# Hybrid decoder block: x2's place as weight buffer twice, the last pair's down in five parts, final_g by DMA, first gate behind two gather groups

## The chip, the cores and the metric

One core of a Trainium2 chip runs the whole program. The metric is the device time of one execution in microseconds; several executions are timed and their median counts. A profile is one execution of its own, with a span (first to last instruction) a little shorter than its device time.

## The reference

One decoder layer on 512 tokens of width 2048, in float32: an attention block (sliding-window heads and forgetting-attention heads) and then a mixture of experts. What matters here is the second half:

```
h2 = rmsnorm(x1, g_moe) * (1 + scale) + shift
group  = top-1 of 4 groups;  expert = top-2 of the 8 experts of that group     # per token
y_e    = (silu(h2 @ w_gate[e]) * (h2 @ w_up[e])) @ w_down[e]                   # 32 experts, 2048 -> 512 -> 2048
x2     = x1 + gate_moe * sum over the token's two experts of weight * y_e
out    = rmsnorm(x2, final_g)
```

The weights of all 32 experts are read once, 12.6 MB for an expert, 403 MB in all.

## The kernel before

The attention block and the router come first. Then 32 experts run in 16 pairs (class `Pair`): the two experts of a pair have up to 64 token slots each and lie side by side in TensorE's columns. Two pairs make a duo (class `Duo`), 8 duos in all. `run_duos` writes the order out by hand, and each engine works in the order of the program.

For a duo the tokens are gathered by matmuls with one-hot matrices (`gather`, tile `xe`), in eight groups of 256 columns of the width. Each group needs its 256 columns of the normed tokens split into a high and a low part first (`split_x`; ScalarE makes the high part, VectorE the low one). The four blocks of a split wait in the list `cuts`, and `step()` runs one of them behind every quarter of a half gate_up; `gather(h)` runs what is left of group h, and at its end asks for the split of a later group. The first duo has three places for splits, so group h + 3 is asked for at the end of gather h.

`gate_up(cc)` multiplies a quarter cc of the width with gate (`pg`, L1345) and up (`pu`), eight matmul pairs each; quarter cc needs groups 2cc and 2cc + 1. In the first duo the order is: gathers 0, 1, 2; gate 0, gather 3, up 0, gather 4; gate 1, gather 5, up 1, gather 6; gate 2, gather 7, up 2; gate 3, up 3. Then `act` and `hid_T` make the hidden rows, `down_rows` (L1367) multiplies them with the down weights, and the sums go back to their tokens by matmuls with the one-hot matrices (`scatter4`, L1389), which VectorE adds into x2 (L1392). The scatters of a pair run between the gate_ups of the next.

Weights come as tiles of [128, 4, 512] float32, 1024 KB: 16 for gate and up and 8 for down in a pair, numbered n = 0 to 383 in the order of their loads. `wload` issues them on SP's queue, a pair ahead of its use, and a load waits until the last reader of its buffer is done. `ring_tile` gives the buffers: two pools of four (`mo`, `rp_`) in turn. Tiles 8 to 11 (quarter 2 of the first pair) take the place of x2, which is not written before the second pair. So tiles 12 to 15 wait for quarter 0, 16 to 19 for quarter 1, 20 to 23 for quarter 3 and so on. All loads are in one queue, in order.

The last pair differs. Its down weights come by column blocks (`down_src`, pieces of 2 KB), the last block in halves. `down` (L1404) multiplies a part of columns (512, 512, 512, 256, 256) with them, VectorE scales it by `gm` (L1409), ScalarE copies the high part (L1414), VectorE makes the remainder (L1415), and four scatters (`scatter`, L1427) for the four token blocks wait in the list `late`; behind each k of the next part `step()` runs one. VectorE adds into x2 (L1429) and ScalarE sums the squares (`last_norm`, L1593). When the last square is in, the root is taken and x2 is scaled with it and with final_g (`fg`, L1604) and stored (L1605). `fg` needs the 2048 values on all 128 partitions: they are loaded as 16 rows of 128 (`fgs`, on ScalarE's queue, at the start of the experts) and spread by 32 matmuls with 16 rows (`fgp`, L1587) and four copies, behind quarter 1 of the last pair.

Of the kernel before, what the change touches and what calls it, by code (L numbers as in the profile page):

```python
# [8 lines left out]
F32 = mybir.dt.float32  # L9
# [8 lines left out]
D = 2048  # L18
TB = 4
# [34 lines left out]
def kernel(  # L54
# [1140 lines left out]
    early = rp_.tile([128, TB, D], F32, tag="x2", name="early")  # L1195
# [81 lines left out]
    def ring_tile():  # L1277

        n = nld[0]
        nld[0] += 1  # L1280
        if 8 <= n < 12:
            return early[:, n - 8, :].rearrange("p (k f) -> p k f", k=4)
        k = n if n < 8 else n - 4
        return (mo, rp_)[k // 4 % 2].tile([128, 4, 512], F32, tag="w", name=f"w{n}", bufs=4)
# [19 lines left out]
    class Pair:  # L1304
# [78 lines left out]
        def scatter4(self, dc, tbs=range(TB)):  # L1383

            sl = slice(dc * 512, (dc + 1) * 512)
            os_ = [ps.tile([128, 512], F32, tag="y", name=f"o_{self.n}_{dc}_{tb}", bufs=4) for tb in tbs]
            for o, tb in zip(os_, tbs):
                for i, v in enumerate(YP[dc % 2]):
                    PE.matmul(o, self.ohT[:, tb, :], v, start=i == 0, stop=i == 1)  # L1389
            for o, tb in zip(os_, tbs):  # L1390
                x2 = total()[:, tb, sl]
                V.scalar_tensor_tensor(x2, o, self.w_col(tb), x2 if self.n else x1[dc][:, tb, :], op0=OP.mult,  # L1392
                                       op1=OP.add)
            if dc < 2 and tbs[-1] == TB - 1:
                self.prepare(dc + 2)

        def down(self, c0, c1):

            dc, sl, w = c0 // 512, slice(c0 % 512, c0 % 512 + c1 - c0), c1 - c0
            name = f"{self.n}_{c0}"  # L1400
            y = ps.tile([128, 512], F32, tag="y", name=f"y_{name}", bufs=4)[:, :w]
            for k in range(4):
# [3 lines left out]
                if 512 <= c0 < 1536:  # L1406
                    step()
            yt = YT[dc % 2][:, sl]
            V.tensor_mul(yt, y, gm[:, c0:c1])  # L1409
            if c1 == D:  # L1410
                parts = (yt,)
            else:
                hi, lo = (t[:, CHUNKS.index((c0, c1)) % 2, :w] for t in XP)
                S.activation(hi, yt, AF.Copy)  # L1414
                V.tensor_sub(lo, yt, hi.bitcast(F32))  # L1415
                parts = (hi, lo)
            if c0 == 1536:
                for _ in range(TB):
                    step()
            late.extend(lambda tb=tb: self.scatter(c0, c1, tb, parts) for tb in range(TB))  # L1420

        def scatter(self, c0, c1, tb, parts):
            o = ps.tile([128, 512], F32, tag="g" if tb % 2 else "y", name=f"o_{self.n}_{c0}_{tb}",
                        bufs=2 if tb % 2 else 4)[:, :c1 - c0]
            oh = self.ohT[:, tb, :]
            for i, v in enumerate(parts):
                PE.matmul(o, oh if len(parts) > 1 else oh.bitcast(F32), v, start=i == 0, stop=i == len(parts) - 1)  # L1427
            x2 = total()[:, tb, c0:c1]
            V.scalar_tensor_tensor(x2, o, self.w_col(tb), x2, op0=OP.mult, op1=OP.add)  # L1429
            self.done((c0, c1), tb)  # L1430
# [63 lines left out]
    def total():  # L1494

        if not x2s:
            x2s.append(rp_.tile([128, TB, D], F32, tag="x2", name="x2"))
        return x2s[0]
# [3 lines left out]
    late, cuts = [], []  # L1502
# [5 lines left out]
    def step():  # L1508

        if late:  # L1510
            late.pop(0)()
        if cuts:
            cut()

    def run_duos(duos, done=None, after=None):
# [3 lines left out]
        for n, (duo, q) in enumerate(order):  # L1519
# [6 lines left out]
            p.done = done if final else None  # L1526
            nxt = duos[duos.index(duo) + 1] if q and not final else None
            if own:
                for h in range(3):
                    duo.gather(h)  # L1530
# [3 lines left out]
            for cc in range(4):  # L1534
                if own:
                    p.gate_up(cc, lambda: duo.gather(2 * cc + 3) if cc < 3 else None)
                    if cc < 2:
                        duo.gather(2 * cc + 4)
# [13 lines left out]
                if cc == 1 and p.done:  # L1552
                    done(None)
# [7 lines left out]
            if p.done:  # L1561
                for cols in CHUNKS:
                    p.down(*cols)
                while late:
                    step()
                return
# [9 lines left out]
    fgs = sm([16, 128], "fgs")  # L1576
    S.dma_start(fgs, final_g.rearrange("(r f) -> r f", r=16))
# [4 lines left out]
    def last_norm(cols, tb=0):  # L1582
        if cols is None:
            for r in range(4):
                t = ps.tile([128, 512], F32, tag="g", name=f"fgp_{r}", bufs=2)
                for k in range(4):
                    PE.matmul(t[:, k * 128:(k + 1) * 128], ident[0:16, 4 * r + k:4 * r + k + 1].to_broadcast([16, 128]),  # L1587
                              fgs, start=True, stop=True)
                S.activation(fg[:, r * 512:(r + 1) * 512], t, AF.Copy)
# [3 lines left out]
        S.activation(HID[:, :c1 - c0], total()[:, tb, c0:c1], AF.Square, accum_out=sf5[:, tb, i:i + 1])  # L1593
# [5 lines left out]
        for tb in range(TB):  # L1599
            y = ring_tile()  # L1600
            for h in range(2):
                sl = slice(h * 1024, (h + 1) * 1024)
                yv = flat(y)[:, sl]
                V.scalar_tensor_tensor(yv, total()[:, tb, sl], rf[:, tb:tb + 1], fg[:, sl], op0=OP.mult, op1=OP.mult)  # L1604
# [114 lines left out]
```

## Time and profile before

| | us |
|---|---|
| three runs | 1917.44, 1919.84, 1924.72 (median 1919.84) |
| profiled execution, device time | 1920.35 |
| its span | 1918.7 |
| TensorE busy in the span | 1811.1 (94%) |
| weight loads of TensorE | 1136.6 (59%) |
| VectorE, ScalarE, GpSimd | 1064.2, 773.5, 342.1 |
| moved by DMA | 572.79 MB |

The mean granted clock of TensorE is 0.981 of full speed. Busy shares are means over stages with different limits; the stages must be read one by one. In the views below, PE is TensorE's matmuls, PEld its weight loads, DVE VectorE, ACT ScalarE, SPq the queue on which SP issues DMAs. L1345 is line 1345 of the kernel. A matmul in the timeline has a start and a modelled end; the spacing of the starts tells more than the durations.

### The profile page before, as it was taken

To read this page: it belongs to the slowest core of one execution; us is meant where nothing else is said; L and a number is where in the kernel's file an instruction comes from. 1 tells how busy PE (TensorE), PEld (TensorE's weight loads), DVE (VectorE), ACT (ScalarE), POOL (GpSimd) and SP (SyncE) were. 2 spreads that over 40 slices of the span, in tenths; PEclk is the share of its full clock that TensorE was granted. 3 is DMA by queue.
4 is the path that set the end of the run, shared out by engine and by line. 5 is a ranking of instruction groups with operands and counts; after the bars stand their busy time and mean duration, and the time that the engine had idled before them with its cause. 6 is when DMAs were issued, how large, how long until landed. Compare 5 with 4: busy or idle time off the path is not lost.

```text
span 1918.7 us, 26373 instructions
## 1 busy us (share of the span) xinstructions
PE 1811.1 (94%) x9801; PEld 1136.6 (59%) x9801; DVE 1064.2 (55%) x1904; ACT 773.5 (40%) x1523; POOL 342.1 (18%) x281
## 2 busy tenths in 40 slices
PE   4998999999999999997999999999999999999994
PEld 2667888787787777776544454444544445444442
DVE  5774666566666545756445455554545545455425
ACT  4445655565555533345423233232332323323113
POOL 2440343443344321454000000000000000000000
PEclk9999999999999899999999999999999999999998
DMA  9993555565566432668699999999999999999993
GB/s 329 325 291 80 162 175 156 163 201 163 170 179 190 120 133 77 216 219 322 234 397 419 421 419 421 420 418 420 418 421 421 417 420 417 421 420 413 421 393 119
DMA packets 208680, 572.79 MB, mean 299 GB/s; under 512 B 22624, under 2 KB 110744, under 8 KB 159904
## 3 DMA queue, kind: packets, MB, share of 16 engines
q1 hardware_dynamic: 207600, 570.95, 79.2%
q8 instruction: 79, 1.29, 0.3%
q14 instruction: 57, 0.47, 0.1%
q10 hardware_dynamic: 944, 0.08, 0.0%
HBM read 566.78 MB, written 4.19 MB: 298 GB/s over the span
## 4 chain that ended last, share of the span: by engine, by line
PE 68%; DMA 7%; ACT 7%; DVE 6%; issue 3%; POOL 1%; SPq 0%; DVEq 0%; ACTq 0%; POOLq 0%
PE pu L1345 11%; PE pg L1345 10%; PE y L1367 9%; PE xe L1479 7%; PE o L1389 5%; DMA w<-in_w_up_dram 5%; PE qp L213 3%; PE qp L215 2%; PE qp L214 2%; DMA raw<-in_w_ada_dram 2%; PE ob L824 1%; PE tb L812 1%; PE vb L214 1%; PE vb L215 1%; PE vb L213 1%
## 5 line engine op out<-in xcount | busy, mean ns | idle before, releaser
L1345 PE MATMUL pu<-w,cw 128*64 128x512 f32 x1008 | 235.9, 593 | 5.9 <-DMA w<-in_w_up_dram 5.9
L1345 PE MATMUL pg<-w,cw 128*64 128x512 f32 x1008 | 235.1, 604 | 0.0
L1488 ACT ACTIVATE cw<-xe,shM,scM 128x128 f32<-128x128 f32 x128 | 58.5, 457 | 427.5 <-PE xe L1479 396.5
L1367 PE MATMUL y<-w,more_f 128*64 128x512 f32 x960 | 217.4, 599 | 4.5 <-ACT xp_whi L1460 2.4
L1486 DVE TENSOR_SCALAR cw<-xe,scM,shM 128x128 f32<-128x128 f32 x128 | 52.5, 410 | 296.9 <-ACT cw L1488 296.9
L623 POOL TENSOR_TENSOR gb<-gb,raw 128x512 f32<-128x512 f32 x112 | 159.6, 1425 | 275.6 <-ACT raw L622 207.2
L1392 DVE SCALAR_TENSOR_TENSOR x<-o,wpair,x 128x512 f32<-128x512 f32 x240 | 163.2, 742 | 26.6 <-PE o L1389 26.6
L1345 PEld LDWEIGHTS pu<-w,cw 128*64 128x64 f32 x1008 | 75.8, 137 | 151.9 <-issue 137.6
L1460 ACT ACTIVATE xp_whi<-x,rs 128x256 fp32r<-128x256 f32 x236 | 162.4, 761 | 1.1 <-DVE rs L133 1.1
L1367 PEld LDWEIGHTS y<-w,more_f 128*64 128x64 f32 x960 | 74.4, 137 | 135.0 <-issue 106.6
L175 DVE TENSOR_TENSOR wlo_s<-raw,whi_s 128x512 fp32r<-128x512 f32 x96 | 89.9, 937 | 109.6 <-ACT whi_s L174 109.5
L1345 PEld LDWEIGHTS pg<-w,cw 128*64 128x64 f32 x1008 | 71.8, 138 | 130.8 <-issue 128.2
L1466 DVE SCALAR_TENSOR_TENSOR xp_wlo<-x,rs,xp_whi 128x256 fp32r<-128x256 f32 x232 | 144.9, 684 | 2.2 <-ACT xp_whi L1460 2.2
L1479 PE MATMUL xe<-cr,xp_whi 128*128 128x256 f32 x472 | 119.8, 294 | 2.4 <-DVE cr L1449 2.4
L620 DVE SCALAR_TENSOR_TENSOR ga<-raw,csil,ga 128x512 f32<-128x512 f32 x112 | 107.9, 963 | 23.1 <-DMA raw<-in_w_ada_dram 22.7
L1479 PEld LDWEIGHTS xe<-cr,xp_whi 128*128 128x128 f32 x472 | 89.8, 190 | 49.5 <-issue 45.4
L1479 PE MATMUL xe<-cr,xp_wlo 128*128 128x256 f32 x472 | 113.7, 281 | 0.3
L213 PE MATMUL qp<-hT_hi,whi_s 128*128 128x512 f32 x256 | 107.3, 419 | 0.0
L215 PE MATMUL qp<-hT_hi,wlo_s 128*128 128x512 f32 x256 | 100.8, 394 | 0.0
L214 PE MATMUL qp<-hT_lo,whi_s 128*128 128x512 f32 x256 | 100.8, 394 | 0.0
L622 ACT ACTIVATE raw<-raw,csil 128x512 f32<-128x512 f32 x112 | 79.7, 714 | 32.1 <-DMA raw<-in_w_ada_dram 23.5
L1479 PEld LDWEIGHTS xe<-cr,xp_wlo 128*128 128x128 f32 x472 | 90.0, 191 | 0.7 <-DVE xp_wlo L1466 0.7
(451 smaller groups left out, 3512.2 us busy)
## 6 DMA issues: line engine op xcount, KB each, us to landing
w<-in_w_gate_dram SPq DMA_DIRECT2D x126, 1024.0 KB, 4.9
w<-in_w_up_dram SPq DMA_DIRECT2D x126, 1024.0 KB, 13.5
w<-in_w_down_dram SPq DMA_DIRECT2D x126, 1024.0 KB, 12.3
raw<-in_w_ada_dram SPq DMA_DIRECT2D x128, 512.0 KB, 4.4
raws<-in_w_ada_dram SPq DMA_DIRECT2D x64, 512.0 KB, 7.0
raw<-in_w_in_dram SPq DMA_DIRECT2D x160, 128.0 KB, 3.0
raw<-in_w_out_dram SPq DMA_DIRECT2D x32, 512.0 KB, 3.8
raw<-in_w_in_dram SPq DMA_DIRECT2D x48, 256.0 KB, 3.4
```

Source lines behind the costliest of these rows:

```text
L213: PE.matmul(o, lhi, rhi, start=first, stop=False, **kw)
L214: PE.matmul(o, lhi, rlo, start=False, stop=False, **kw)
L215: PE.matmul(o, llo, rhi, start=False, stop=last, **kw)
L620: V.scalar_tensor_tensor(a, ts[n][:, j, :], s, a, op0=OP.mult, op1=OP.add)
L623: G.tensor_add(a, a, ts[n][:, j, :])
L1345: PE.matmul(o[64 * e:64 * e + 64, :], self.xe(cc)[:, j, 64 * e:64 * e + 64], w[cc, e][:, j, :], start=cc == 0 and j == 0, stop=cc == 3 and ...
L1367: PE.matmul(ys[dc][64 * e:64 * e + 64, :], HT[:, k, 64 * e:64 * e + 64], self.wd[k, e][:, dc, :], start=k == 0, stop=k == 3)
L1389: PE.matmul(o, self.ohT[:, tb, :], v, start=i == 0, stop=i == 1)
L1392: V.scalar_tensor_tensor(x2, o, self.w_col(tb), x2 if self.n else x1[dc][:, tb, :], op0=OP.mult, op1=OP.add)
L1460: S.activation(hi[tb], xv, AF.Identity, scale=s)
L1466: V.scalar_tensor_tensor(lo[tb], xv, s, hi[tb].bitcast(F32), op0=OP.mult, op1=OP.subtract)
L1479: PE.matmul(t[:, j, :], v[tb][:, j, :], OHS[:, tb].rearrange("p q s -> p (q s)"), start=tb + i == 0, stop=tb + i == TB)
```

## The change

Four things. First, x2's place is cut into four tiles, one for each block of 128 tokens, and it takes weight tiles twice: 8 to 11 as before and 20 to 23 (the second half of the first pair's down). Later tiles keep the ring of eight, so 24 to 31 take the buffers of 12 to 19. Second, the last pair's down and its scatters are no longer woven matmul by matmul: part i + 1 is multiplied, then the scatters of part i follow together (`last_y`, `last_o`), then the adds and squares. Third, final_g is loaded onto all partitions by one DMA on SP, issued as the last pair starts; the 16-row load, the 32 matmuls and the four copies go. Fourth, in the first duo the first gate starts behind two gathers: gathers 0, 1; gate 0, gather 2, up 0, gather 3; gate 1, gather 4, up 1, gather 5; gate 2, gather 6, up 2, gather 7; gate 3, up 3.

```diff
--- before.py
+++ after.py
@@ -1192,7 +1192,6 @@
     rp_ = ctx.enter_context(tc.tile_pool(name="wring", bufs=1, side="right", reuse_waits="tile"))
-    early = rp_.tile([128, TB, D], F32, tag="x2", name="early")
@@ -1278,9 +1277,9 @@
         n = nld[0]
         nld[0] += 1
-        if 8 <= n < 12:
-            return early[:, n - 8, :].rearrange("p (k f) -> p k f", k=4)
-        k = n if n < 8 else n - 4
+        if 8 <= n < 12 or 20 <= n < 24:
+            return rp_.tile([128, 4, 512], F32, tag=f"x2{n % 12 - 8}", name=f"w{n}")
+        k = n if n < 8 else n - 4 if n < 20 else n - 8
         return (mo, rp_)[k // 4 % 2].tile([128, 4, 512], F32, tag="w", name=f"w{n}", bufs=4)
@@ -1388,46 +1387,45 @@
-                x2 = total()[:, tb, sl]
+                x2 = total(tb)[:, sl]
-        def down(self, c0, c1):
-            dc, sl, w = c0 // 512, slice(c0 % 512, c0 % 512 + c1 - c0), c1 - c0
-            name = f"{self.n}_{c0}"
-            y = ps.tile([128, 512], F32, tag="y", name=f"y_{name}", bufs=4)[:, :w]
+        def last_y(self, i):
+            c0, c1 = CHUNKS[i]
+            dc, w = c0 // 512, c1 - c0
+            sl = slice(c0 % 512, c0 % 512 + w)
+            y = ps.tile([128, 512], F32, tag="y", name=f"y_{self.n}_{c0}", bufs=4)[:, :w]
             for k in range(4):
                 for e in range(2):
                     PE.matmul(y[64 * e:64 * e + 64, :], HT[:, k, 64 * e:64 * e + 64], self.wd[dc, e][:, k, sl],
                               start=k == 0, stop=k == 3)
-                if 512 <= c0 < 1536:
-                    step()
-            yt = YT[dc % 2][:, sl]
+            yt = YT[i % 2][:, :w]
             V.tensor_mul(yt, y, gm[:, c0:c1])
             if c1 == D:
-                parts = (yt,)
-            else:
-                hi, lo = (t[:, CHUNKS.index((c0, c1)) % 2, :w] for t in XP)
-                S.activation(hi, yt, AF.Copy)
-                V.tensor_sub(lo, yt, hi.bitcast(F32))
-                parts = (hi, lo)
-            if c0 == 1536:
-                for _ in range(TB):
-                    step()
-            late.extend(lambda tb=tb: self.scatter(c0, c1, tb, parts) for tb in range(TB))
-        def scatter(self, c0, c1, tb, parts):
-            o = ps.tile([128, 512], F32, tag="g" if tb % 2 else "y", name=f"o_{self.n}_{c0}_{tb}",
-                        bufs=2 if tb % 2 else 4)[:, :c1 - c0]
-            oh = self.ohT[:, tb, :]
-            for i, v in enumerate(parts):
-                PE.matmul(o, oh if len(parts) > 1 else oh.bitcast(F32), v, start=i == 0, stop=i == len(parts) - 1)
-            x2 = total()[:, tb, c0:c1]
-            V.scalar_tensor_tensor(x2, o, self.w_col(tb), x2, op0=OP.mult, op1=OP.add)
-            self.done((c0, c1), tb)
+                return (yt,)
+            hi, lo = (t[:, i % 2, :w] for t in XP)
+            S.activation(hi, yt, AF.Copy)
+            V.tensor_sub(lo, yt, hi.bitcast(F32))
+            return hi, lo
+        def last_o(self, i, parts):
+            c0, c1 = CHUNKS[i]
+            os_ = [ps.tile([128, 512], F32, tag="g" if tb % 2 else "y", name=f"o_{self.n}_{c0}_{tb}",
+                           bufs=2 if tb % 2 else 4)[:, :c1 - c0] for tb in range(TB)]
+            for tb in range(TB):
+                oh = self.ohT[:, tb, :]
+                for k, v in enumerate(parts):
+                    PE.matmul(os_[tb], oh if len(parts) > 1 else oh.bitcast(F32), v, start=k == 0,
+                              stop=k == len(parts) - 1)
+            for tb in range(TB):
+                x2 = total(tb)[:, c0:c1]
+                V.scalar_tensor_tensor(x2, os_[tb], self.w_col(tb), x2, op0=OP.mult, op1=OP.add)
+                self.done((c0, c1), tb)
@@ -1491,15 +1489,15 @@
     x2s = []
-    def total():
+    def total(tb):
         if not x2s:
-            x2s.append(rp_.tile([128, TB, D], F32, tag="x2", name="x2"))
-        return x2s[0]
+            x2s.extend(rp_.tile([128, D], F32, tag=f"x2{i}", name=f"x2_{i}") for i in range(TB))
+        return x2s[tb]
     CHUNKS = ((0, 512), (512, 1024), (1024, 1536), (1536, 1792), (1792, D))
-    late, cuts = [], []
+    cuts = []
@@ -1507,8 +1505,6 @@
     def step():
-        if late:
-            late.pop(0)()
         if cuts:
             cut()
@@ -1524,18 +1520,20 @@
                 succ = d.pairs[i]
                 succ.load(n + 2 == len(order))
             p.done = done if final else None
+            if p.done:
+                done(None)
             nxt = duos[duos.index(duo) + 1] if q and not final else None
             if own:
-                for h in range(3):
+                for h in range(2):
                     duo.gather(h)
             elif nxt:
                 nxt.choose()
                 nxt.split_x(0)
             for cc in range(4):
                 if own:
-                    p.gate_up(cc, lambda: duo.gather(2 * cc + 3) if cc < 3 else None)
-                    if cc < 2:
-                        duo.gather(2 * cc + 4)
+                    p.gate_up(cc, lambda: duo.gather(2 * cc + 2) if cc < 3 else None)
+                    if cc < 3:
+                        duo.gather(2 * cc + 3)
                 else:
                     p.gate_up(cc, lambda: prev.scatter4(2) if final and cc == 2 else None)
                 if cc == 3:
@@ -1549,8 +1547,6 @@
                         prev.scatter4(cc, range(TB) if cc < 3 else range(2))
                     elif cc == 2:
                         prev.scatter4(3)
-                if cc == 1 and p.done:
-                    done(None)
             if after and own:
                 after()
             if p.done:
@@ -1559,10 +1555,11 @@
             if prev and not final:
                 prev.scatter4(3, range(2, TB))
             if p.done:
-                for cols in CHUNKS:
-                    p.down(*cols)
-                while late:
-                    step()
+                parts = [p.last_y(0)]
+                for i in range(1, 6):
+                    if i < 5:
+                        parts.append(p.last_y(i))
+                    p.last_o(i - 1, parts[i - 1])
                 return
@@ -1573,24 +1570,17 @@
-    fgs = sm([16, 128], "fgs")
-    S.dma_start(fgs, final_g.rearrange("(r f) -> r f", r=16))
     fg = cw[:, 0:2048]
     sf5 = sm([128, TB, 5], "sf5")
     sf, rf, tf = sm([128, TB], "sf"), sm([128, TB], "rf"), sm([128, TB], "tf")
     def last_norm(cols, tb=0):
         if cols is None:
-            for r in range(4):
-                t = ps.tile([128, 512], F32, tag="g", name=f"fgp_{r}", bufs=2)
-                for k in range(4):
-                    PE.matmul(t[:, k * 128:(k + 1) * 128], ident[0:16, 4 * r + k:4 * r + k + 1].to_broadcast([16, 128]),
-                              fgs, start=True, stop=True)
-                S.activation(fg[:, r * 512:(r + 1) * 512], t, AF.Copy)
+            SP.dma_start(fg, bcast(final_g, D))
             return
         c0, c1 = cols
         i = CHUNKS.index(cols)
-        S.activation(HID[:, :c1 - c0], total()[:, tb, c0:c1], AF.Square, accum_out=sf5[:, tb, i:i + 1])
+        S.activation(HID[:, :c1 - c0], total(tb)[:, c0:c1], AF.Square, accum_out=sf5[:, tb, i:i + 1])
         if c1 < D or tb < 3:
             return
@@ -1601,7 +1591,7 @@
             for h in range(2):
                 sl = slice(h * 1024, (h + 1) * 1024)
                 yv = flat(y)[:, sl]
-                V.scalar_tensor_tensor(yv, total()[:, tb, sl], rf[:, tb:tb + 1], fg[:, sl], op0=OP.mult, op1=OP.mult)
+                V.scalar_tensor_tensor(yv, total(tb)[:, sl], rf[:, tb:tb + 1], fg[:, sl], op0=OP.mult, op1=OP.mult)
                 SP.dma_start(out[tb * 128:(tb + 1) * 128, sl], yv)
     pairs = [Pair(a * 8 + e, (16 * a + e, 16 * a + 8 + e),
```

## Rows read from the trace of the kernel before

**Rows 1.** The page of the profiled execution, part 2: the span in 40 equal slices of 48 us, TensorE's busy tenths and what the DMA engines moved (GB/s).

```profile
PE   4998999999999999997999999999999999999994
...
GB/s 329 325 291 80 162 175 156 163 201 163 170 179 190 120 133 77 216 219 322 234 397 419 421 419 421 420 418 420 418 421 421 417 420 417 421 420 413 421 393 119
```

**Rows 2.** The waits of TensorE's weight loads (PEld) from 960 to 1870 us, the groups of `pu` that waited for the sequencer's issue and for landings of `w_up` (us in total, times, longest), and three of these loads in the timeline (start, us; in brackets the idle time before it and what ended it).

```profile
PEld pu L1345 <- issue: 131.9, 465, 0.4
...
PEld pu L1345 <- DMA w<-in_w_up_dram: 13.1, 9, 1.8
...
1101.40 0.20 PEld L1345 LDWEIGHTS pu<-w,cw 128*64 128x64 f32 x4 [1.74 <-DMA w<-in_w_up_dram]
...
1221.66 0.20 PEld L1345 LDWEIGHTS pu<-w,cw 128*64 128x64 f32 x4 [1.75 <-DMA w<-in_w_up_dram]
...
1833.61 0.20 PEld L1345 LDWEIGHTS pu<-w,cw 128*64 128x64 f32 x4 [0.83 <-DMA w<-in_w_up_dram]
```

**Rows 3.** A window of 10 us in the first pair (length, busy us of each engine with instructions, granted TensorE clock, DMA share, GB/s).

```profile
950.00:960.00 10.00, 9.13 (x48) 3.13 (x44) 1.43 (x7) 2.45 (x4) 0.00 (x0) 1.00 0.42 150
```

**Rows 4.** The timeline of SP's queue: issues of weight tiles, merged (start, us from the first to the last issue, count).

```profile
920.82 0.80 SPq L1291 DMA_DIRECT2D w<-in_w_gate_dram  x2
...
933.08 26.04 SPq L1291 DMA_DIRECT2D w<-in_w_down_dram  x8
966.82 1.69 SPq L1291 DMA_DIRECT2D w<-in_w_gate_dram  x2
...
981.73 0.80 SPq L1291 DMA_DIRECT2D w<-in_w_gate_dram  x2
...
1026.18 0.80 SPq L1291 DMA_DIRECT2D w<-in_w_gate_dram  x2
```

**Rows 5.** The chain of waits, in order of time, in the last pair (start, us, engine, tile and line).

```profile
1839.31 4.32 PE fgp L1587 x32
1843.62 6.41 PE pg L1345 x16
...
1857.72 3.58 PE pg L1345 x16
...
1866.96 3.68 PE y L1404 x16
```

**Rows 6.** The timeline of TensorE in the first pair's gathers (`xe`) and its first gate, and VectorE's split of the fourth group.

```profile
915.16 0.29 PE L1479 MATMUL xe<-cr,more_r 128*128 128x256 f32 x1
...
917.14 3.65 PE L1345 MATMUL pg<-w,cw 128*64 128x512 f32 x16
920.72 0.39 PE L1479 MATMUL xe<-cr,xp_whi 128*128 128x256 f32 x1
...
921.63 0.28 PE L1479 MATMUL xe<-cr,xp_whi 128*128 128x256 f32 x1
922.03 0.38 PE L1479 MATMUL xe<-cr,xp_wlo 128*128 128x256 f32 x1
...
923.25 3.65 PE L1345 MATMUL pu<-w,cw 128*64 128x512 f32 x16
...
919.33 2.65 DVE L1466 SCALAR_TENSOR_TENSOR xp_wlo<-x,rs,xp_whi 128x256 fp32r<-128x256 f32 x4 [0.24 <-ACT xp_whi L1460]
```

**Rows 7.** The window from pair 1's first weight issue to pair 2's.

```profile
966.82:1026.18 59.36, 59.02 (x302) 27.92 (x300) 33.33 (x56) 21.90 (x35) 0.00 (x0) 1.00 0.99 404
```

**Rows 8.** Windows of half a microsecond behind the issue of tile 14 at 926.93 into an idle queue.

```profile
927.50:928.00 0.50, 0.50 (x4) 0.30 (x2) 0.50 (x1) 0.00 (x0) 0.00 (x0) 1.00 0.01 0
928.00:928.50 0.50, 0.38 (x4) 0.36 (x4) 0.09 (x1) 0.00 (x0) 0.00 (x0) 1.00 0.63 131
```

**Rows 9.** Windows of the last pair, and SP's last two weight issues in the timeline.

```profile
1845.00:1850.00 5.00, 5.00 (x15) 1.22 (x11) 0.00 (x0) 0.00 (x0) 0.00 (x0) 0.57 0.98 403
1850.00:1855.00 5.00, 5.00 (x24) 2.45 (x24) 2.73 (x4) 0.00 (x0) 0.00 (x0) 1.00 0.92 321
...
1853.50:1872.00 18.50, 16.40 (x76) 5.83 (x70) 4.11 (x6) 3.29 (x5) 0.00 (x0) 1.00 1.04 373
...
1866.08 3.46 SPq L1325 DMA_DIRECT2D w<-in_w_down_dram  x2
```

**Rows 10.** The timeline of the tail: product and copy of a 512-column part, y of 256 columns, four adds of a part, squares, eight adds of 256 columns, the last sum and the scaling.

```profile
1870.66 0.69 DVE L1409 TENSOR_TENSOR cw<-y,gm 128x512 f32<-128x512 f32 x1 [5.10 <-PE y L1404]
1871.39 0.63 ACT L1414 ACTIVATE xp_whi<-cw 128x512 fp32r<-128x512 f32 x1 [4.48 <-DVE cw L1409]
...
1886.67 1.95 PE L1404 MATMUL y<-w,more_f 128*64 128x256 f32 x16
...
1890.75 2.72 DVE L1429 SCALAR_TENSOR_TENSOR x<-o,wpair,x 128x512 f32<-128x512 f32 x4
...
1891.59 0.63 ACT L1593 ACTIVATE cw<-x 128x512 f32<-128x512 f32 x1 [1.21 <-DVE x L1429]
...
1893.88 3.23 DVE L1429 SCALAR_TENSOR_TENSOR x<-o,wpair,x 128x256 f32<-128x256 f32 x8
...
1894.61 0.42 ACT L1593 ACTIVATE cw<-x 128x256 f32<-128x256 f32 x1
...
1898.94 0.17 DVE L1596 TENSOR_REDUCE sf<-sf 128x4 f32<-128x20 f32 x1 [1.84 <-ACT cw L1593]
...
1900.60 9.66 DVE L1604 SCALAR_TENSOR_TENSOR w<-x,rf,cw 128x1024 f32<-128x1024 f32 x8
```

## The prediction

> **What bounds the kernel now.** I read the page's 40 slices first. From slice 21 to 38 the DMA engines move nearly the same 420 GB/s in every slice, and TensorE (PE) is busy too [rows 1]. This is the expert stage: 16 pairs of experts, 24 weight tiles of 1.05 MB (1024 KB) each, 384 in all. Two engines are therefore full at once, and the question is which of them ends last. The waits of PE's weight loads answer it: in the whole stage they waited for a landing of `w_up` 9 times, 13.1 us in all, the typical one 1.74 us at the second half of a gate_up [rows 2]. Between loads there is about 0.29 us of issue anyway (131.9 us in 465 times), so a wait loses some 1.45 us, once per duo (two pairs). The wait comes back every 1221.66 - 1101.40 = 120.26 us [rows 2], so PE alone would need some 118.7 for a duo. DMA binds, by little: the stream's position sets the end, but PE can gain at most 13.1 - 9 x 0.29 = 10.5 us in the stage before it is the bound itself.
>
> Next, where the stream is not full: slices 18 to 20 [rows 1], and 150 GB/s in the window from 950 to 960 [rows 3]. SP's issues say why. Twelve tiles are asked for ahead of the first gather; tiles 12 and 13 wait until the first gate releases its buffers at 920.82, and so on. The eight down tiles are issued over 26 us from 933.08, because four of them wait for the gate_up of the last quarter. Only from 966.82 do issues come faster than transfers [rows 4].
>
> Last, the end. Behind the wait at 1833.61 [rows 2] PE waits for no tile. The chain of waits there is PE alone: 4.32 us of `fgp` (final_g spread by matmuls), then one gate of 6.41 us where the next takes 3.58 [rows 5].
>
> **Part 1: two gather groups ahead of the first gate.** The same matmuls run, in another order. A gather with its inputs ready takes 917.14 - 915.16 = 1.98 us. The gather behind the first gate runs from 920.72 to 923.25, 2.53 us, with a hole between 921.63 and 922.03: its last block is split by VectorE until 921.98 [rows 6]. That split was asked for only one half gate_up earlier. After the change every such gather comes one half gate_up later than its split, so the hole closes. Five gathers times 0.5 us: the first pair ends 2.5 us earlier, and each gate up to the third starts 2 to 4 us earlier. Bounds: 0, if the splits stay the limit, to 2.7.
>
> **Part 2: x2's place twice.** Tiles 20 to 23 (down, k = 2 and 3) wait for the third quarter's gate_up instead of the fourth's, and 24 to 31 each take the wait of four tiles before. At most the stream gains four tiles: at 420 GB/s a tile takes 2.5 us, so 10 us. It can't keep that. The ring is eight tiles in the steady state, before and after, so a lead lasts only as long as SP is never out of tiles to ask for. From 966.82 to the first issue of pair 2 at 1026.18 SP issued 24 tiles, 25.17 MB [rows 4]; the queue moved 404 GB/s x 59.36 us = 23.98 MB [rows 7]. So 1.19 MB, 2.8 us, lay waiting at that point. A tile issued into an idle queue shows no bytes in 927.50 to 928.00 after its issue at 926.93 and a third of the rate in the next half microsecond [rows 8], a start of some 1.3 us. The spare is thus 1.5 to 2.8 us. With a larger lead the queue runs dry at this point and waits for PE. As PE comes 2.5 us earlier (part 1), the tile of 1026.18 can land 1.5 + 2.5 = 4.0 to 2.8 + 2.5 = 5.3 us earlier; I take **4.5**. The bounds are 0 (no lead held) and 7.6 (tile 32 could be asked for at 981.73 - 2.5 = 979.2, and the stream now reaches it at 966.82 + 8 x 2.5 = 986.8, if nothing limited it later [rows 4]).
>
> Does PE follow? It starts 2.5 us earlier, the stream 4.5, so PE has 2.0 us in hand. The first duo's wait of 1.5 to 1.65 vanishes, the second's shrinks, and from the third on PE waits as before, all 4.5 us earlier. That is less than the 2.5 + 10.5 us at which PE would bind. No other engine waits for x2: pair 1 first adds into it behind its own first gate_up, when the down rows that read tiles 20 to 23 are long done. SP's queue is in order, and behind the four issues stand only loads that are needed later.
>
> [...]
>
> **Part 3: final_g by DMA.** Removed: 4.32 us of `fgp` on PE, four copies on an idle ScalarE and a small load on its queue. [...] Added: one 1 MB load on SP, issued behind the last weight tile. Today's last weight issue ends at 1866.08 + 3.46 = 1869.5 [rows 9]; behind it on SP stand only the stores of the result. Its consumer is the scaling at 1900.60 [rows 10], so it lies beside the tail.
>
> [...]
>
> PE now reaches the last pair's down 4.5 + 7.15 = 11.65 us earlier, at 1866.96 - 11.65 = 1855.3. Is the stream there? In 2 KB pieces it moves 373 GB/s [rows 9], 2.8 us per tile. Its gate tiles are in by some 1853 now (the rate falls to 321 GB/s in 1850 to 1855, where the queue runs out for a moment [rows 9]), so by 1848.5; four down tiles more take 11.2, so part 2's tiles land at about 1859.7. The second y could start at 1855.3 + 3.45 = 1858.75: **it waits 1.0 us**, and later parts don't.
>
> **Part 4: the last down in five parts.** From first y to last square it is now 1898.94 - 1866.96 = 31.98 us [rows 5, 10]. I walk the new order with row durations: y 3.45 (3.70 until seen), y of 256 columns 1.95, scatter of four 2.05, product 0.69, copy 0.63, remainder 0.69 like the product, four adds 2.72 (256: 3.23 / 2), and by their spacing a square (1894.61 - 1891.59) / 4 = 0.75, of 256 columns (1898.94 - 1894.61) / 8 = 0.54 [rows 10]; first y = 0. y1 is seen at 8.15, its remainder ready at 10.25; VectorE works in order, so part 0's adds run 10.25 to 12.97. y2 seen 13.7; product, copy, remainder to 15.8; adds of part 1 to 18.5. Product of y3 to 18.95, its copy behind part 1's squares at 19.55, remainder to 20.45; adds of part 2 to 23.17; product of y4 to 23.60; adds of part 3 to 25.20, of part 4 to 26.80. Squares of part 3 end at 26.4, those of part 4 at **28.6**. Gain 3.4 us, the wait of 1.0 included. Bounds: 0 (VectorE's order costs as much as PE's holes now) to 6 (PE alone: 3.45 + 2.05 per full part).
>
> **Sum.** 4.5 + 7.15 + 3.4 = 15.05 us. The profiled execution took 1920.35 us (span 1918.7 and 1.65 around it): 1905.3. It lies 0.5 above the median of 1919.84, so the median forecast is 1904.8, **1905**.
>
> **Rivals.** (a) The lead isn't held: the queue runs dry at 1026 because the first pair is no faster. The sum loses 4.5: 1909.3. For it: the spare is only 2.8 us at most. Against: the holes in the gathers are plain. (b) The tail is no shorter, as VectorE and ScalarE are in order: 1908.2. With (a) it is 1912.7. (c) The clock falls in the last pair anyway: 1907.6. (d) More lead and a PE-bound tail: 4.5 + 3 and 3.4 + 2.5, so 1899.3. (e) The other side: final_g arrives late. All 128 partitions read one 8 KB row. If these packets are served one after another, each takes as long as a packet of a weight tile now has on its engine, 2.5 us / 8 = 0.31 us, and 128 of them 40 us; queued behind the last tile at 1871.5 they end at 1911.5 instead of the 1900.6 at which scaling starts now: about 11 us slower, 1931. It decides from 30 us on. Against: the reads go to 16 engines, and the load has 10 us to spare at the ordinary rate. (f) The change does not do what it says: SP might hold tiles 20 to 23 to the old wait; that is (a).
>
> **Chances.** Forecast with its own bounds (1901.5 to 1907.5) 0.55; (a) 0.10, (b) 0.09, both 0.09; (c) 0.04; (d) 0.08; (e) 0.05. Faster by over 0.5% means below 1910.2; 0.5% is about what a measurement here can tell from no change. Faster: 0.55 + 0.10 + 0.09 + 0.04 + 0.08 less a twentieth for their upper ends, 0.82; same: the case of both and those ends, 0.13; slower 0.05. Range 1900 to 1911: it leaves out (e), most of the case of both and the end of (d).
>
> **What will show it.** Right: no hole in the gathers behind the gates; issues of tiles 20 to 23 near 941 and 947; pair 2's first issue near 1023.7 with the rate in pair 1 below 420 GB/s; PE without a `w_up` wait in the first duo, and with one again from the third; no fall of the clock near 1835 to 1845; first y near 1855, first square sum near 1884, scaling near 1885.6 without a DMA wait. Wrong: duo waits gone to the end (more lead than I allow), or unchanged from the first; a half clock in the last pair; VectorE idle for final_g.

## The result, and the profile after

| | median us | runs | lowest to highest |
|---|---|---|---|
| before | 1919.82 | 6 | 1916.23 to 1924.72 |
| after | 1906.04 | 6 | 1904.80 to 1908.37 |

The ratio is 0.9927 with a 95% interval of 0.9911 to 0.9944: 14.0 us less (10.7 to 17.1) of 1919.8. The forecast was 1905. The profiled execution took 1905.22 us, its span 1903.5.

Where did the time go? The first view is the page's row of GB/s in 40 slices [rows 1].

```profile
GB/s 326 329 297 75 156 178 155 157 204 166 188 172 188 122 133 67 213 198 288 354 360 391 421 420 420 420 419 420 420 420 420 419 420 420 417 421 415 420 413 215
```

Slice 20 was a hole at 234 and is 354 now, and slices 21 and 22 stay below 420 (360 and 391): the stream is ahead and has nothing to catch up. SP's queue shows the cause [rows 4]; these are the timelines of the changed kernel, TensorE's first gather and SP's issues of weight tiles (start, us from first to last issue, count).

```profile
911.28 0.55 PE L1477 MATMUL xe<-cr,xp_whi 128*128 128x256 f32 x1 [2.39 <-DVE cr L1447]
```

```profile
931.85 17.74 SPq L1290 DMA_DIRECT2D w<-in_w_down_dram  x8
...
954.46 0.80 SPq L1290 DMA_DIRECT2D w<-in_w_gate_dram  x2
...
1024.04 0.80 SPq L1290 DMA_DIRECT2D w<-in_w_gate_dram  x2
```

The eight down tiles go out in 17.74 us, not 26.04, and the next pair's first two at 954.46, not 966.82. The first gather of the kernel before stands here:

```profile
909.06 0.55 PE L1479 MATMUL xe<-cr,xp_whi 128*128 128x256 f32 x1 [2.38 <-DVE cr L1449]
```

So the experts began 2.22 us later in the profile after. Nothing of the change lies ahead of that point, and in the other traces of this study it comes between 906.75 and 914.81 with no pattern by edit. **Traces are therefore compared from the first gather on.** The tile issued at 1026.18 before, the third pair's first, was issued 117.12 us behind it and is at 112.76 now. It landed at 124.33 and lands at 117.56, 6.77 us earlier.

A part of that was not in the sum. TensorE's timeline of the first pair's down, first of before, then of after:

```profile
961.45 15.65 PE L1367 MATMUL y<-w,more_f 128*64 128x512 f32 x64 [1.62 <-ACT more_f L1359]
```

```profile
961.04 13.95 PE L1366 MATMUL y<-w,more_f 128*64 128x512 f32 x64 [1.62 <-ACT more_f L1358]
```

The same 64 matmuls take 1.70 us less: in before the granted clock reads 0.50 in every half microsecond from 962.0 to 965.0. Windows of 10 us (length, busy us of PE, PEld, DVE, ACT, POOL, granted clock, DMA share, GB/s); before, then after:

```profile
960.00:970.00 10.00, 8.55 (x32) 2.75 (x34) 1.79 (x12) 0.90 (x3) 0.00 (x0) 0.83 0.86 332
```

```profile
960.00:970.00 10.00, 8.96 (x42) 3.07 (x44) 1.62 (x11) 0.69 (x2) 0.00 (x0) 1.00 1.00 398
```

The last pair, by the chain of waits of after [rows 5] and a window of 5 us [rows 9]:

```profile
1834.71 3.58 PE pg L1344 x16
...
1845.98 3.58 PE pg L1344 x16
1849.57 3.48 PE pu L1344 x16
...
1855.23 4.50 PE y L1404 x18
1859.77 3.65 PE y L1404 x14
```

```profile
1845.00:1850.00 5.00, 5.00 (x25) 1.95 (x25) 2.35 (x4) 0.36 (x1) 0.00 (x0) 1.00 1.01 391
```

No `fgp`, no gate of 6.41, clock 1.00. The second y breaks after two matmuls: its weight load waits 0.9 us for a landing of `w_down`. The tail [rows 10], in VectorE's timeline and one row of SP's:

```profile
1875.28 0.42 DVE L1412 TENSOR_TENSOR xp_wlo<-more_f,xp_whi 128x256 fp32r<-128x256 f32 x1 [1.11 <-ACT xp_whi L1411]
1875.62 2.72 DVE L1427 SCALAR_TENSOR_TENSOR x<-o,wpair,x 128x512 f32<-128x512 f32 x4
...
1878.59 3.22 DVE L1427 SCALAR_TENSOR_TENSOR x<-o,wpair,x 128x256 f32<-128x256 f32 x8
1883.80 0.17 DVE L1586 TENSOR_REDUCE sf<-sf 128x4 f32<-128x20 f32 x1 [1.99 <-ACT cw L1583]
...
1885.45 3.68 DVE L1594 SCALAR_TENSOR_TENSOR w<-x,rf,cw 128x1024 f32<-128x1024 f32 x3
```

```profile
1863.03 2.14 SPq L1579 DMA_DIRECT2D cw<-in_final_g_dram  x1
```

Final_g is asked for at 1863 and the scaling at 1885.45 has no wait for it. From first y to last sum: 1883.80 - 1855.23 = 28.57, before 31.98. From the first gather to the first y: 943.95, before 957.90. So 957.90 - 943.95 = 13.95 and 31.98 - 28.57 = 3.41 were won, 17.36, less the late start of 2.22: 15.1 between the two profiled executions.

### The profile page after: what moved, and what is told of

It reads as the page before. It is cut to its first block, busy times and chain, and to the rows that moved or that the text cites. A ratio compares the mean times of both kernels' runs of the same rounds, so it can differ in the third digit from the quotient of the medians.

```text
span 1903.5 us, 26308 instructions
## 1 busy us (share of the span) xinstructions
PE 1798.6 (94%) x9769; PEld 1130.6 (59%) x9769; DVE 1062.5 (56%) x1904; ACT 771.3 (41%) x1519; POOL 342.5 (18%) x281
## 4 chain that ended last, share of the span: by engine, by line
PE 70%; DMA 6%; ACT 6%; DVE 5%; issue 3%; POOL 1%; SPq 0%; DVEq 0%; ACTq 0%; POOLq 0%
PE pu L1344 12%; PE pg L1344 11%; PE y L1366 9%; PE xe L1477 7%; PE o L1388 5%; DMA w<-in_w_up_dram 4%; PE qp L213 2%; PE qp L215 2%; PE qp L214 2%; DMA raw<-in_w_ada_dram 1%; PE ob L824 1%; PE tb L812 1%; ACT raw L622 1%; PE vb L214 1%; ACT whi_s L174 1%
## 5 line engine op out<-in xcount | busy, mean ns | idle before, releaser
L1344 PE MATMUL pu<-w,cw 128*64 128x512 f32 x1024 | 240.1, 593 | 5.0 <-DMA w<-in_w_up_dram 5.0
L1477 PE MATMUL xe<-cr,xp_whi 128*128 128x256 f32 x472 | 119.6, 294 | 2.4 <-DVE cr L1447 2.4
L1477 PEld LDWEIGHTS xe<-cr,xp_whi 128*128 128x128 f32 x472 | 89.8, 190 | 49.5 <-issue 45.4
```

What stands on the lines that cost most here:

```text
L1344: PE.matmul(o[64 * e:64 * e + 64, :], self.xe(cc)[:, j, 64 * e:64 * e + 64], w[cc, e][:, j, :], start=cc == 0 and j == 0, stop=cc == 3 and ...
L1477: PE.matmul(t[:, j, :], v[tb][:, j, :], OHS[:, tb].rearrange("p q s -> p (q s)"), start=tb + i == 0, stop=tb + i == TB)
```

## The experiments

Medians of the kernel before: 1919.15 (31 runs) beside the four single parts (e1 to e4), 1920.08 (17) beside e5, e12 and e9, 1920.34 (11) beside e7 and e8. A ratio below is the recorded one of the two sets of runs, with its 95% interval; it isn't exactly the quotient of the two medians. A saving by ratio is one less the ratio, times the median of before.

**Each part alone.** The theory is the prediction's sum; the rivals are in the texts.

```diff
 # e1: part 3 alone, in the kernel before
-    fgs = sm([16, 128], "fgs")
-    S.dma_start(fgs, final_g.rearrange("(r f) -> r f", r=16))
...
+            SP.dma_start(fg, bcast(final_g, D))
```

> The kernel before with part 3 alone (final_g by DMA). My theory: the 32 matmuls of 4.3 us go and the half clock behind them goes too (2.8 us), so the first y of the last pair comes 7.1 us earlier and the tail stays at 32.0 us: time 1912.7, granted clock 1.00 in the last pair's gates. Rival (the fall has another cause): 4.3 us earlier only, one gate still 6.4 us, 1915.5. Rival (the load of final_g is late): scaling waits for a DMA, 1920 or more.

```diff
 # e2: part 4 alone
-                for cols in CHUNKS:
-                    p.down(*cols)
+                parts = [p.last_y(0)]
...
```

> The kernel before with part 4 alone (five parts, scatters one part later); final_g still by matmuls. My theory: first y to last square sum 27.7 us (no wait for tiles here) to 28.6 instead of 32.0: 1915.5 to 1916.4. Rival (VectorE's and ScalarE's order costs what PE's holes cost): 31 to 32 us, 1919 to 1920.

```diff
 # e3: part 2 alone
-        if 8 <= n < 12:
+        if 8 <= n < 12 or 20 <= n < 24:
...
-        k = n if n < 8 else n - 4
+        k = n if n < 8 else n - 4 if n < 20 else n - 8
```

> The kernel before with part 2 alone (x2's place takes tiles 20 to 23 too). My theory (a lead is kept only up to the spare at pair 2's first weight issue plus what PE comes earlier): the stage from the first gather on gets 1.5 to 2.8 us shorter, pair 2's first issue stays where it is against the first gather (117.1 us), rate below 420 GB/s in pair 1: 1917 to 1918.3. Rival (buffers alone make the lead, four tiles): 7 to 10 us shorter, 1910 to 1913. Rival (no lead held at all): 1919.8.

```diff
 # e4: part 1 alone
-                for h in range(3):
+                for h in range(2):
...
-                    p.gate_up(cc, lambda: duo.gather(2 * cc + 3) if cc < 3 else None)
+                    p.gate_up(cc, lambda: duo.gather(2 * cc + 2) if cc < 3 else None)
...
```

> The kernel before with part 1 alone (first gate behind two gathers). My theory: the gathers' holes close, the first pair's issues and with them the whole stream come 2.5 to 2.7 us earlier: 1917.2, pair 2's first issue 114.5 us after the first gather. With the down of the first pair at full clock, as in the changed kernel's profile, 4.3 us: 1915.5. Rival (the stream is bound by bytes, PE's head start is lost): 0, 1919.8.

```diff
 # e5: parts 1 and 2, the edits of e3 and e4 together
```

> Parts 1 and 2 alone (the gathers in the new order, and x2's place used twice), with the old tail and final_g over TensorE as before. Alone the two gave 2.9 and 1.9 us. If they simply add, 1914.3 us; my prediction's term for both, 4.5, says 1914.6. If the two help each other, as the trace of the whole change suggests (the first product of the last pair's down 6.9 us earlier, counted from the first gather and without final_g's 7.1), 1912.3 us. In the trace, counted from the first gather: the third pair's first weight issue at 112.8 (before: 117.1), and its landing near 117.6 (before: 124.3). Whether final_g's matmuls are followed by the half clock in this execution is open: the first two single edits that kept those matmuls had it in one of three profiled executions.

```diff
 # e12: the changed kernel once more, no edit
```

> The changed kernel once more, beside the same runs of the kernel before as the others of this call, to be the measure for the two: 1906.0 us. If the four single edits add up (5.1 + 3.2 + 1.9 + 2.9 = 13.1) it stands at 0.9932 of the kernel before; if the lead grows when the two edits of the first pair come together, at 0.992 or lower.

```diff
 # e7: the changed kernel without part 1
-                for h in range(2):
+                for h in range(3):
...
```

> The changed kernel with part 1 undone (the first duo's gathers in the old order). By the single edits the gathers are worth 2.9 us; by the pair of edits (5.6) less x2's alone (1.9), 3.7. So the ratio to the kernel before rises from 0.9928 to 0.9943 (simple sum) or 0.9947 (the two help each other); with neither, if the gathers only help when x2's place is not used twice, it stays at 0.9928. In the trace the third pair's first weight issue comes again 117 us after the first gather (112.8 with both). The clock of the first pair's down, 0.83 over 10 us in all six traces that have at most one of the two edits and full in the four that have both, tells something too: 0.83 again if it hangs on the edits, either if it hangs on when the stretch comes.

```diff
 # e8: the changed kernel without the second use of x2's place
-        if 8 <= n < 12 or 20 <= n < 24:
+        if 8 <= n < 12:
...
-        k = n if n < 8 else n - 4 if n < 20 else n - 8
+        k = n if n < 8 else n - 4
```

> The changed kernel with part 2's use undone (tiles 20 to 23 wait for places of the ring again; x2 is still four tiles). Simple sum: 1.9 us lost, 0.9938 of the kernel before; by the pair of edits less the gathers alone, 2.7, 0.9942. In the trace the third pair's first weight issue near 115 us after the first gather and its landing 8 us behind the issue (4.8 with both), so that the earlier issue is eaten by transfers that queue. The clock of the first pair's down as in the other run.

Measured, with four columns from the timelines (TensorE's first `xe`, SP's issue of tile 48, the first y of the last pair, VectorE's last sum); tile 48 is the third pair's first:

| kernel | median us | ratio to before (95%) | first gather to tile 48 issued / landed | to first y | first y to last sum | first pair's down | `fgp` + next gate |
|---|---|---|---|---|---|---|---|
| before | | | 117.1 / 124.3 | 957.90 | 31.98 | 15.65 | 10.73 |
| e1, part 3 | 1914.05 | 0.9968 (0.9958 to 0.9978) | 117.1 / 123.9 | 950.39 | 31.96 | 15.65 | none |
| e2, part 4 | 1915.98 | 0.9979 (0.9970 to 0.9988) | 116.9 / 123.5 | 957.13 | 27.48 | 15.44 | 10.72 |
| e3, part 2 | 1917.21 | 0.9993 (0.9982 to 1.0004) | 117.4 / 122.5 | 953.18 | 31.97 | 15.65 | 7.39 |
| e4, part 1 | 1916.22 | 0.9983 (0.9974 to 0.9992) | 115.1 / 123.2 | 952.94 | 31.98 | 15.31 | 7.40 |
| e5, parts 1, 2 | 1914.47 | 0.9966 (0.9955 to 0.9978) | 113.5 / 118.4 | 951.92 | 31.98 | 13.95 | 10.71 |
| e7, all but 1 | 1909.05 | 0.9937 (0.9921 to 0.9953) | 115.4 / 120.2 | 946.55 | 28.57 | 13.95 | none |
| e8, all but 2 | 1907.52 | 0.9934 (0.9917 to 0.9950) | 112.5 / 119.6 | 945.67 | 28.88 | 13.96 | none |
| e12, all | 1904.90 | 0.9928 (0.9910 to 0.9946) | 112.7 / 117.8 | 944.29 | 28.59 | 13.96 | none |

Three things follow.

The parts add up, within intervals of some 2 us each. By ratio the single ones give 6.1, 4.0, 1.3 and 3.3 us, 14.7, and the whole 14.0 and 13.8. (By the medians the single ones are 5.1, 3.2, 1.9 and 2.9, the figures that the later expectations use.) Part 2's 1.3 isn't clear of nothing (-0.8 to 3.5), but its rival of 7 to 10 us is out. The interval of e1 (4.2 to 8.1) holds its theory, 7.1, and its rival, 4.3; its trace decides below.

That parts 1 and 2 need each other isn't shown. In the landing of tile 48 it looks so: part 2 alone lands it 1.85 us earlier without issuing it earlier, part 1 alone issues it 2.1 earlier and lands it 1.1 earlier, and both together (e5) land it 6.0 earlier. But e5 has the full clock in the first pair's down (1.00 over 10 us), and e3 and e4 don't (0.83). e7 and e8 have it too (1.00), and there tile 48 was not issued 117 and 115 us after the first gather, as expected, but 115.4 and 112.5. Among the kernels without `fgp`, the time to the first y falls from e1's by 3.8 us with part 2 (e7), 4.7 with part 1 (e8) and 6.1 with both (e12). Each of the three holds the 1.70 of the clock once, so the two parts would add to 3.8 + 4.7 - 1.7 = 6.8, and together they give less. The times don't decide. By ratio e7 lost 1.7 us against e12 and e8 1.2, less than the 2.9 and 1.9 of the simple sum, but their intervals hold the simple sum, mutual help and no loss at all.

Third, the fall of the clock at `fgp`, which the 7.15 of the prediction's sum takes as given, did not come in e3 and e4. In windows of 5 us from the block on, before has a granted clock of 0.82, 0.50 and 0.99, e3 and e4 have 1.00 in all three. The chain of waits of e3 has

```profile
1841.33 3.81 PE fgp L1586 x32
1845.15 3.58 PE pg L1344 x16
```

where [rows 5] has 4.32 and 6.41. That calls for a closer test. In e1, without `fgp`, the clock is full too (1.00); its window:

```profile
1845.00:1850.00 5.00, 5.00 (x23) 2.00 (x22) 2.21 (x4) 0.00 (x0) 0.00 (x0) 1.00 1.01 417
```

**What lowers the clock.** The three kernels below do extra matmuls whose results are not used. They stand in pairs 1 to 14 (counted from 0), all between the first pair and the last.

```diff
 # e10: final_g's 32 matmuls in the 14 pairs between as well (small copies to a scratch tile)
-                if cc == 1 and p.done:
-                    done(None)
+                if cc == 1 and done and (p.done or not own):
+                    done(None if p.done else 0)
...
```

> The kernel before with final_g's 32 matmuls (16 rows each) and four small copies repeated at the same place in each of the 14 pairs between the first duo and the last pair; only the last pair's are used. Theory that the half clock behind them depends on when they come: some of the 15 blocks, between a third and two thirds, are followed by a granted clock near 0.5 for 3 to 4 us (block 4.3 us, next group 6.4), the others not (block 3.8, next group 3.6). Rival, my prediction's term (the matmuls always cost 2.8 us of clock behind them): all 15. Second rival (the fall has nothing to do with them): one at most. The time is 1919 plus 14 times 3.8 to 7.1 us where TensorE sets the pace, 1972 to 2018, less what the weights leave it to wait now (12.3 us).

```diff
 # e11: e10 with 128 rows, 112 of them zero
...
+    V.memset(fgs, 0.0)
...
-                    PE.matmul(..., ident[0:16, 4 * r + k:4 * r + k + 1].to_broadcast([16, 128]), fgs, ...)
+                    PE.matmul(..., ident[:, 4 * r + k:4 * r + k + 1].to_broadcast([128, 128]), fgs, ...)
```

> As the run with final_g's 32 matmuls in each of the pairs, but final_g's tile has 128 rows, 112 of them zero, so that each matmul reads 128 rows and not 16; columns, count and durations stay. Theory that the 16 rows lower the clock: no block is followed by a fall, each takes 3.8 us and the next group 3.6, and the time is about 1919.5 + 14 x 3.8 - 12.3 = 1960 us. Rival, that the rows do not matter (128 columns in 270 ns each are what lowers it): 1995 us and falls behind all 15 as in that run.

```diff
 # e13: e10, but in the 14 pairs eight matmuls behind each quarter
+                elif done and not final and not own:
+                    done(0, cc)
...
```

> As the run with final_g's matmuls in each of the pairs, but in the 14 added places they come eight at a time (about 1 us), one block after each of the pair's four gate groups; the last pair's 32 stay together. Theory that a fall needs the narrow matmuls in one stretch: none behind the blocks of eight, 1919.5 + 14 x 3.8 - 12.3 = 1960 us. Rival, that each narrow block can lower the clock: falls behind a share of them, 1980 us or more.

| kernel | us, one run | blocks of 32 with a fall behind them |
|---|---|---|
| e10 | 1994.59 | 15 of 15 |
| e11 | 1957.19 | 0 of 15 |
| e13 | 1959.51 | the last pair's one; none behind the 56 blocks of eight |

One window from 1000 to 1800 us for each, e10, e11, e13 in turn; the number ahead of the last two is the mean granted clock:

```profile
1000.00:1800.00 800.00, 797.93 (x4030) 394.87 (x4028) 375.23 (x618) 230.70 (x420) 0.00 (x0) 0.96 0.95 386
```

```profile
1000.00:1800.00 800.00, 797.61 (x4210) 402.20 (x4208) 396.37 (x653) 244.89 (x443) 0.00 (x0) 1.00 0.99 403
```

```profile
1000.00:1800.00 800.00, 800.00 (x4167) 394.60 (x4167) 390.20 (x647) 244.53 (x441) 0.00 (x0) 1.00 0.97 399
```

TensorE reads as busy in all three. So in these runs it is behind matmuls of 16 rows that the clock fell, behind 32 in a row and not behind eight at a time: in the second 5 us from a block's start the granted clock is 0.50 to 0.58 (nine blocks) or 0.75 to 0.81 (six) in e10, and 1.00 at all 15 in e11; in e13 it is 1.00 in every window of 5 us from 990, the first block of eight, to 1880. (e10 ran on another chip than e11 and e13, but the last block of e13, 32 with 16 rows, had a fall on e11's chip.) My expectation for e10 was wrong in its shares: a fall came behind every block, in two sizes. From its chain of waits, one of each, and one block of e11:

```profile
1072.77 4.28 PE fgp L1589 x32
1077.05 6.39 PE pg L1345 x16
```

```profile
1136.93 3.76 PE fgp L1589 x32
1140.69 5.28 PE pg L1345 x16
```

```profile
1133.01 3.57 PE fgp L1590 x32
1136.59 3.58 PE pg L1345 x16
```

Block and gate take 10.67 (nine of the 15) or 9.04 (six), against 7.39 in e3 with no fall: prices of 3.28 and 1.65. For the 14 added blocks, nine large and five small, that makes 37.8 us; e10 is 37.4 above e11. That is a rough agreement of two single executions: a block of e11 is also 0.2 us shorter than one of e3. In the last pair of the seven traces that have the block there, the fall was large in three (before and e2 with 0.50, e5 with 0.54 in the second 5 us), small in two (e10 with 0.76, e13 with 0.67) and absent in two (e3, e4, with 1.00).

**A shorter tail.** VectorE waits 1.11 us for part 3's copy at 1875.28 (above), which stands behind four squares on ScalarE.

```diff
 # e9: the changed kernel, part 3 in plain float32 as well
-            if c1 == D:
+            if i >= 3:
                 return (yt,)
```

> The changed kernel with the fourth of the last pair's five parts (columns 1536 to 1792) scattered in plain float32, as the fifth already is, in place of a split into two halves. In the trace of the changed kernel the adds of that part wait for the copy of its high half (it ends at 1875.26, on ScalarE behind the squares of the second part) and for the remainder (0.42 us). Theory: that copy and that remainder are on the path that sets the end, so the last sum comes 0.8 to 1.5 us earlier and the time is 1904.7 us. Rival: the matmuls in float32 take the place of the wait (TensorE has about as much left to do), or the squares on ScalarE set the end whatever the copy does: 1906 us, no difference.

1902.16 us (1900.39 to 1905.51, 5 runs), ratio 0.9913 (0.9896 to 0.9930), beside 1904.90 for e12. The intervals of the two ratios overlap, so the times alone don't show it faster than the changed kernel. In the trace it takes 27.24 us from first y to last sum, not 28.57: 1.3 us, as expected. The other 1.4 us of the medians' difference has no cause in the trace. ScalarE's timeline there begins the squares at

```profile
1868.39 0.63 ACT L1583 ACTIVATE cw<-x 128x512 f32<-128x512 f32 x1 [1.48 <-DVE x L1427]
...
1874.56 0.42 ACT L1583 ACTIVATE cw<-x 128x256 f32<-128x256 f32 x1 [0.16 <-DVE x L1427]
```

and waits between them only once, for 0.16 us: the squares bind the tail now.

## Why the prediction was right, and where it was not

The forecast of 1905 held by its own steps; two terms were off, one up and one down.

| term | forecast us | traces | runs, by ratio |
|---|---|---|---|
| lead of parts 1 and 2 | 4.5 | 6.0 (e5), 6.8 (after) | e5: 6.5 (4.2 to 8.6) |
| final_g | 7.15 | 7.1 with the large fall, 5.5 with the small, 3.8 with none | e1: 6.1 (4.2 to 8.1) |
| tail with the wait for y1 | 3.4 | 3.41 | |
| tail without that wait | 4.4 | 4.50 (e2) | e2: 4.0 (2.3 to 5.8) |
| the wait for y1 (first two y, after less e2) | 1.0 | 8.18 - 7.09 = 1.09 | |

**The lead** was mis-sized by a step that the sum did not have. At tile 48 it is 6.77: the earlier issue, 4.36, and a landing 2.42 us sooner behind its issue (7.22 to 4.80). The forecast had 2.5 for the first and 2.0 for the second, the spare. The spare was well bounded (1.5 to 2.8; here 2.42, in e3 1.85). Of the 4.36, 1.70 is the first pair's down at full clock, and the remaining 2.66 is the gathers' term. That term isn't constant. In the six traces with the new order the first pair's down begins 49.5 to 50.6 us after the first gather (52.4 before), so it is 1.8 to 2.9. In the five of them with a window there it is the smaller, the lower the granted clock in the 10 us from the first gather on: 0.72 in e4 (1.81 us), 0.73 in e5 (1.92), 0.75 in e9 (2.02), 0.82 in e12 (2.65) and in the changed kernel (2.63). The windows of e4 and of the changed kernel:

```profile
910.09:920.09 10.00, 10.00 (x48) 7.37 (x48) 7.48 (x15) 5.64 (x12) 0.00 (x0) 0.72 0.66 272
```

```profile
911.28:921.28 10.00, 10.00 (x54) 7.34 (x55) 8.31 (x16) 6.22 (x12) 0.00 (x0) 0.82 0.66 271
```

So the mechanism holds: the lead is PE's gain plus the spare, and no more, though four tiles would be 10 us. Part 2 alone gave 1.3 us (at most 3.5), and PE's waits for `w_up` are still there, 12.3 us in 11 waits of `pu`'s loads in the changed kernel. The measurement decides against four tiles' worth.

Is the full clock in the first pair's down a gift of the edits? That stays open. Ahead of it TensorE waits 1.62 us for ScalarE in both views above, and as long in all fourteen traces, so that wait alone doesn't decide. The down took 15.31 to 15.65 us in seven traces and 13.95 or 13.96 in seven: the longer time in five of the six with neither part 1 nor part 2, in two of the four with one of them, in none of the four with both. But e13, which leaves that stretch as it was, has it full (13.95, at 1.00), and so a full clock there doesn't need the edits. Without it the lead would be 5.1 in the trace of after (6.77 - 1.70) and 4.3 in e5 (5.98 - 1.70), around the forecast.

**final_g.** The 7.15 of the sum is the 4.32 of `fgp` and the 6.41 - 3.58 = 2.83 that the gate behind it takes more [rows 5], at a granted clock of 0.57 from 1845 to 1850 [rows 9] (0.50 in every half microsecond from 1842.5 to 1849.0). That the 16-row matmuls lower the clock was an inference from this one window; it is now shown by e10 (0.96 from 1000 to 1800) against e11 (1.00), and in e1's trace the gate (3.58) and the clock (1.00) are full without them. Taking the loss as certain was too much: 2.83 behind the block is right for executions with the large fall (three of seven traces), and the average over executions is less. Rival (c), that the clock falls anyway, is out: e1 and the changed kernel have 1.00 there, and the gates of the last pair take 3.58 in all six traces without `fgp`. PE reads no less busy in the fall: 5.00 of 5.00 us in e10 from 1077.70 to 1082.70, at a clock of 0.50. What makes the fall behind a last block large, small or none, as in the seven traces, is not shown by any run here.

**The tail** came out as walked, wait included. **Rivals.** (a) and (f) fall with e5, (b) with e2; (d) falls as the duo waits are back and the tail is what was forecast; (e) falls with the scaling that waits for nothing. In the loads' timeline the first of these waits fell from 1.74 us [rows 2] to 0.26. The prediction had the second shrink too, but it is back at 1.72, and so is the one at 1819.03:

```profile
1097.39 0.19 PEld L1344 LDWEIGHTS pu<-w,cw 128*64 128x64 f32 x3 [0.26 <-DMA w<-in_w_up_dram]
...
1217.07 0.20 PEld L1344 LDWEIGHTS pu<-w,cw 128*64 128x64 f32 x4 [1.72 <-DMA w<-in_w_up_dram]
...
1819.03 0.20 PEld L1344 LDWEIGHTS pu<-w,cw 128*64 128x64 f32 x4 [1.72 <-DMA w<-in_w_up_dram]
```

The close agreement has luck in it: of what the traces show, 2.3 us more lead stand against 2.22 us of a later start in the one profile, and in the medians the same surplus stands against falls that do not always come.

Two readings in the prediction are slightly off and change nothing: slice 21 reads 397 GB/s, not 420 [rows 1], and 131.9 us in 465 times is 0.28 us of issue, not 0.29 [rows 2].

## What to carry to other kernels

Price a buffer edit at the point where the queue runs dry: the lead that survived here (6.77 us) was the consumer's own gain (4.36) plus what still lay waiting there (2.42), not the size of the buffers. Look for narrow matmuls ahead of a stretch at half clock; spreading them or filling their rows was enough here (granted clock 1.00 in e13 and e11, 0.96 in e10). Before two edits are said to help each other, see that the clock is the same in the traces that are compared. Count traces from the first instruction of the stage that was changed, and take a clock loss seen once as a chance, not as a constant.

## What was not expected of the hardware

Matmuls of 128 columns with 16 rows and with 128 rows have nearly the same duration (270 and 275 ns median), yet 32 of the first in a row cost up to 3.28 us of clock (e10) and 32 of the second nothing (e11, clock 1.00 at all 15 blocks), though 112 of their rows were zeros. Eight at a time (1.15 us) cost no clock either (e13, 1.00). And the same 64 matmuls of the first pair's down took 15.65 or 13.95 us in executions of different kernels that do not differ there (before and e13).
